# Per-head norm with the log read from PSUM, and a guard before the second up weight load, in a decoder trunk on one core

## Chip, cores and metric

One Trainium2 (trn2) chip, one core. The metric is device time in microseconds (us) of one execution of the program. Times of the whole kernel are the median over runs; durations of single instructions come from one execution that the hardware profiler recorded.

## What is computed

One decoder layer over 1024 tokens of width 1024, all in float32. Cut to what matters:

```
h = rms_norm(x, norm_mix_g);  z = h @ w_in                 # 512 pooling columns, then q, k, v of 4 heads
y_pool = pooling_mixer(z[..., :512])                       # trailing windows 2, 4, 8, 16, then a map per group
o = diff_attention(q, k, v, lam, rel_bias)                 # two softmax maps per head, 128 value channels per head
o = rms_norm(o, subln_g, 1e-5) * (1.0 - lam_init)          # the per-head norm, over the 128 channels of a head
x = x + concat(y_pool, o) @ w_out
h = rms_norm(x, norm_ffn_g);  gu = h @ ffn_w_in            # 2 x 2816 columns
x = x + (silu(causal_conv3(gu[:, :2816])) * gu[:, 2816:]) @ ffn_w_out
out = rms_norm(x, norm_final_g)
```

## The kernel before

All matrix products are made in two-part precision: an operand is split into a rounded part (hi) and the rest (lo), and three matmuls (hi x hi, hi x lo, lo x hi) stand for one. The split is a cast on ScalarE (lines 79 and 83) and a subtraction on GpSimd or VectorE (lines 80 and 84). P is 128.

The kernel runs in stages. Row norms of x and transposes come first, then the projections of q, k, v and of the pooling groups, interleaved with attention by a list written out by hand (`PLAN`, line 37). `attention(h, j)` (line 373) does 256 tokens of head h: two softmax maps, transposes, the split of the weights (ah, al), and the product with v into the PSUM tile "pv". The kernel keeps eight PSUM tiles (lines 65 to 75): three "sc", two "tp", two "mm" and a single "pv", called a bank below. At every odd j, 512 tokens of the head are complete, and their per-head norm follows (lines 411 to 430): a Square on ScalarE, a split, two matmuls with a matrix of ones that put the sum of squares on all partitions (tile ss, also in the "pv" bank), the variance, r = exp(-0.5 ln(variance)), one Newton step for r on VectorE, and the scaling of yT by r and gsub. There are eight such norms.

Then the output projection runs in three groups of channel blocks (`OUT_PLAN`, line 39); the rows wander through device memory (x1_d) between the groups. In the third group (lines 602 to 610) each row tile t is finished, normed by `norm2(t)` (line 577 scales it in place), and each pair of row tiles is turned into seven blocks (b11, b21, b22, t1 to t4) by `pair_blocks` (line 587): subtractions on GpSimd, for the last pair mostly on VectorE, then transposes on TensorE and splits. These blocks are operands of a Strassen-like scheme: for each of 22 channel tiles `ffn_up` (line 656) makes seven products of 12 matmuls, in the order 1, 6, 7, 5, 2, 4, 3. `up_weights(ct)` (line 616) loads the two weight tiles ru and rg of a channel tile into two buffers ("rw", line 619), issues both on SP's queue (line 621), forms their sums and differences on GpSimd and VectorE (lines 628 to 631) and splits them. It is called for tile ct + 1 before the products of tile ct, and for tile 0 before the loop (lines 689 to 694). The tiles gt and the split of sb take the four "x" buffers that held the row tiles. At the end comes the down projection `ffn_down`, with the last norm in `finish`.

The program is written without explicit order among engines: `TileContext(nc, schedule_with_timeline_sim=True)` (line 822) orders each engine's instructions when the program is built, by priority and by a simulated timeline, and sets the semaphores. Once built, each engine runs its instructions in that fixed order. A `tc.high_priority()` block is put ahead where it can be.

Of the kernel before, what the change touches and what calls it, by code (L numbers as in the profile page):

```python
# [9 lines left out]
F32 = mybir.dt.float32  # L10
F32R = mybir.dt.float32r
AF = mybir.ActivationFunctionType
ALU = mybir.AluOpType
PSUM = bass.MemoryType.PSUM

P = 128
S = 1024
D = 1024
KC = D // P
NT = S // P  # L20
# [5 lines left out]
SUB_EPS = 1e-5  # L26
LAM_INIT = 0.8 - 0.6 * math.exp(-0.3 * 0)
# [15 lines left out]
def trunk_kernel(ctx, tc, x, norm_mix_g, w_in, pool_w, rows, line, rel_bias, w_out, norm_ffn_g,  # L43
                 ffn_w_in, ffn_w_out, norm_final_g, onehot, out):
    nc = tc.nc
# [7 lines left out]
    const = ctx.enter_context(tc.tile_pool(name="const", bufs=1))  # L53
# [5 lines left out]
    att = st_att.enter_context(tc.tile_pool(name="att", bufs=1))  # L59
    ps_a = ctx.enter_context(tc.tile_pool(name="ps_a", bufs=1, space=PSUM))  # L60

    def slot(dt, name):
        return slots.tile([P, S], dt, tag="y", name=name)

    def sc_ps(name):
        return ps_a.tile([P, 512], F32, tag="sc", bufs=3, name=name)
# [121 lines left out]
    prm = const.tile([P, 96], F32, name="prm")  # L188
    gsub = const.tile([P, 1], F32, name="gsub")
    nlam = const.tile([P, 1], F32, name="nlam")  # L190

    def small_params():
        r_ps = sc_ps("r_ps")
        nc.tensor.matmul(r_ps[0:NH, :], rb, oh, start=True, stop=True)
        r_sb = att.tile([NH, 512], F32, tag="vt", bufs=1, name="r_sb")
        nc.vector.tensor_copy(r_sb, r_ps[0:NH, :])
        nc.sync.dma_start(scratch, r_sb)
        prm_ps = sc_ps("prm_ps")
        nc.tensor.transpose(prm_ps[:, 0:93], prow[0:93, :], ident[0:93, 0:93])
        nc.vector.tensor_copy(prm[:, 0:93], prm_ps[:, 0:93])  # L200
        nc.vector.tensor_scalar(gsub, prm[:, 92:93], 1.0 - LAM_INIT, None, op0=ALU.mult)
        nc.vector.tensor_copy(recfar, flat[:, 256:276])
        lam_s = const.tile([P, 2], F32, name="lam_s")
        lam_p = att.tile([P, 64], F32, tag="tb", bufs=1, name="lam_p")
        for j in range(2):
            nc.vector.tensor_tensor_reduce(lam_p, lam_in[:, 2 * j, :], lam_in[:, 2 * j + 1, :], 1.0, 0.0,
                                           ALU.mult, ALU.add, lam_s[:, j:j + 1])
        lam_e = const.tile([P, 2], F32, name="lam_e")
        nc.scalar.activation(lam_e, lam_s, AF.Exp)
        nc.vector.tensor_tensor(nlam, lam_e[:, 1:2], lam_e[:, 0:1], op=ALU.subtract)  # L210
        nc.vector.tensor_scalar(nlam, nlam, -LAM_INIT, None, op0=ALU.add)
# [109 lines left out]
    for t in range(NT):  # L321
# [9 lines left out]
        sq = att.tile([P, S], F32, tag="pl", bufs=3, name=f"sq_{t}")  # L331
        r = row_rstd(xt, sq, f"m{t}")
# [40 lines left out]
    def attention(h, j):  # L373
        tb, (q, kh, kl, vh, vl) = bias[h], qkv[h]
        if j == 0:
            yT[4 + h] = slot(F32, f"yT{4 + h}")
        y = yT[4 + h]
        a = []
        for i in (2 * j, 2 * j + 1):
            w = (i + 1) * P  # L380
            negm = small.tile([P, 2], F32, tag="negm", name=f"nm{h}_{i}")
            sums = small.tile([P, 2], F32, tag="sums", name=f"sm{h}_{i}")
            s = [att.tile([P, S], F32, tag="p", bufs=4, name=f"p{h}_{i}_{c}") for c in range(2)]
            for c in range(2):
                softmax_map(h, tb, i, c, q, kh, kl, s[c], negm, sums)
            r = small.tile([P, 2], F32, tag="rcp", name=f"rc{h}_{i}")
            nc.vector.reciprocal(r, sums)
            nc.vector.tensor_scalar(r[:, 1:2], r[:, 1:2], nlam, None, op0=ALU.mult)
            nc.scalar.mul(s[1][:, 0:w], s[1][:, 0:w], r[:, 1:2])
            nc.vector.scalar_tensor_tensor(s[0][:, 0:w], s[0][:, 0:w], r[:, 0:1], s[1][:, 0:w],  # L390
                                           op0=ALU.mult, op1=ALU.add)
            if i % 2 == 0:
                nc.gpsimd.memset(s[0][:, w:w + P], 0.0)
            a.append(s[0])
        nk = 2 * j + 2
        pv = pv_ps(f"pv{h}_{j}")
        for kp in range(nk // 2):
            tp = tp_ps(f"tpa{h}_{j}_{kp}")
            for u in range(2):
                for v in range(2):  # L400
                    k = 2 * kp + u
                    nc.tensor.transpose(tp[:, 2 * u + v, :], a[v][:, k * P:(k + 1) * P], ident)  # L402
            ah = att.tile([P, 4, P], F32R, tag="ah", bufs=2, name=f"ah{h}_{j}_{kp}")
            al = att.tile([P, 4, P], F32R, tag="al", bufs=2, name=f"al{h}_{j}_{kp}")
            psplit(ah, al, tp)
            for u in range(2):
                k = 2 * kp + u
                mm3(pv[:, 0:256], vh[:, k, :], vl[:, k, :], ah[:, 2 * u:2 * u + 2, :],
                    al[:, 2 * u:2 * u + 2, :], k == 0, k == nk - 1)
        nc.scalar.copy(y[:, j * 256:(j + 1) * 256], pv[:, 0:256])  # L410
        if j % 2:
            cs = slice((j // 2) * 512, (j // 2) * 512 + 512)
            n = f"{h}_{j}"
            sq = att.tile([P, 512], F32, tag="ln", bufs=2, name=f"sq{n}")
            nc.scalar.activation(sq, y[:, cs], AF.Square)
            sh = att.tile([P, 512], F32R, tag="ah", bufs=2, name=f"sqh{n}")
            sl = att.tile([P, 512], F32R, tag="al", bufs=2, name=f"sql{n}")
            split(sh, sl, sq)
            ss = pv_ps(f"ss{n}")
            nc.tensor.matmul(ss, ones, sh, start=True, stop=False)  # L420
            nc.tensor.matmul(ss, ones, sl, start=False, stop=True)
            var = att.tile([P, 512], F32, tag="ln", bufs=2, name=f"va{n}")
            nc.vector.tensor_scalar(var, ss, 1.0 / P, SUB_EPS, op0=ALU.mult, op1=ALU.add)
            r = att.tile([P, 512], F32, tag="al", bufs=2, name=f"r{n}")
            nc.scalar.activation(r, var, AF.Ln)
            nc.scalar.activation(r, r, AF.Exp, scale=-0.5)
            nc.vector.tensor_tensor(sq, r, r, op=ALU.mult)
            nc.vector.scalar_tensor_tensor(sq, sq, -0.5, var, op0=ALU.mult, op1=ALU.mult)
            nc.vector.scalar_tensor_tensor(r, sq, 1.5, r, op0=ALU.add, op1=ALU.mult)
            nc.vector.scalar_tensor_tensor(y[:, cs], y[:, cs], gsub, r, op0=ALU.mult, op1=ALU.mult)  # L430


# [54 lines left out]
    bias = {}  # L487
# [40 lines left out]
    x1 = [None] * NT  # L528
# [87 lines left out]
    def up_weights(ct):  # L616
        raw = []
        for n, c in (("u", NCT + ct), ("g", ct)):
            r = mid.tile([P, KC * P], F32, tag="rw", bufs=2, name=f"r{n}{ct}")
            src = ffn_w_in[:, c * P:(c + 1) * P].rearrange("(k p) c -> p k c", p=P)  # L620
            nc.sync.dma_start(r.rearrange("p (k c) -> p k c", c=P), src)
            raw.append(r)
        u, g = raw
        a11, a12, a21, a22 = u[:, 0:512], u[:, 512:1024], g[:, 0:512], g[:, 512:1024]
        sa = mid.tile([P, S], F32, tag="st", bufs=2, name=f"sa{ct}")
        sb = mid.tile([P, S], F32, tag="st", bufs=2, name=f"sb{ct}")
        s1, s2, s3, s4 = sa[:, 0:512], sa[:, 512:1024], sb[:, 0:512], sb[:, 512:1024]
        nc.gpsimd.tensor_tensor(s1, a21, a22, op=ALU.add)  # L628
        nc.vector.tensor_tensor(s2, s1, a11, op=ALU.subtract)  # L629
        nc.vector.tensor_tensor(s4, a12, s2, op=ALU.subtract)  # L630
        nc.gpsimd.tensor_tensor(s3, a11, a21, op=ALU.subtract)
        uh, ul = u_tile(F32R, f"uh{ct}"), u_tile(F32R, f"ul{ct}")
        split(uh, ul, u)
        gt = x_tile(F32R, f"gt{ct}")
        split(gt[:, 0:512], gt[:, 512:1024], a22, nc.vector)
        sh = []
        for n, t in (("a", sa), ("b", sb)):
            h, l = (u_tile if n == "a" else x_tile)(F32R, f"s{n}h{ct}"), u_tile(F32R, f"s{n}l{ct}")
            split(h, l, t, nc.vector)
            sh.append((blocks(h), blocks(l)))  # L640
        (ah, al), (bh_, bl_), (uh, ul), gb = sh[0], sh[1], (blocks(uh), blocks(ul)), blocks(gt)
        return {"1": (uh[:, 0], ul[:, 0], "b11"), "2": (uh[:, 1], ul[:, 1], "b21"), "3": (bh_[:, 1], bl_[:, 1], "b22"),
                "4": (gb[:, 0], gb[:, 1], "t4"), "5": (ah[:, 0], al[:, 0], "t1"), "6": (ah[:, 1], al[:, 1], "t2"),
                "7": (bh_[:, 0], bl_[:, 0], "t3")}
# [112 lines left out]
    ct = 0  # L757
# [68 lines left out]
```

## Time and profile before

| | |
|---|---|
| median of 3 runs | 1113.54 us |
| lowest and highest run | 1113.40 and 1116.36 us |
| the profiled execution | 1115.49 us |
| its span in the profile | 1113.7 us |
| TensorE granted clock, mean over the span | 0.987 |

Engines are named PE (TensorE matmul), PEld (its weight load), DVE (VectorE), ACT (ScalarE), POOL (GpSimd) and SP (SyncE, which here only issues transfers); a q behind a name is that engine's queue. Times within the span count from its start. A line number such as L621 is the line of the kernel that issued an instruction; where a helper issues it, as the splits on lines 79, 80, 83 and 84, the tile names tell which use it is. "out<-in" gives the tiles, without their numbers. What stands in brackets at the end of a row of the timeline is how long the engine was idle before the instruction, and what ended that.

### The profile page before, as it was taken

To read this page: it belongs to the slowest core of one execution; us is meant where nothing else is said; L and a number is where in the kernel's file an instruction comes from. 1 tells how busy PE (TensorE), PEld (TensorE's weight loads), DVE (VectorE), ACT (ScalarE), POOL (GpSimd) and SP (SyncE) were. 2 spreads that over 40 slices of the span, in tenths; PEclk is the share of its full clock that TensorE was granted. 3 is DMA by queue.
4 is the path that set the end of the run, shared out by engine and by line. 5 is a ranking of instruction groups with operands and counts; after the bars stand their busy time and mean duration, and the time that the engine had idled before them with its cause. 6 is when DMAs were issued, how large, how long until landed. Compare 5 with 4: busy or idle time off the path is not lost.

```text
span 1113.7 us, 13597 instructions
## 1 busy us (share of the span) xinstructions
PE 1066.6 (96%) x5011; PEld 884.0 (79%) x5011; DVE 732.3 (66%) x1213; ACT 475.9 (43%) x775; POOL 341.7 (31%) x240
## 2 busy tenths in 40 slices
PE   5999999999899997999999999999999999999997
PEld 4988888887677675878888888888888788888885
DVE  7556787877797689577657656755665655544545
ACT  5557476655752355244333443443344222111133
POOL 3232242433730247133312232221314322221211
PEclk9999999999899998999999999999999999999999
DMA  8010110110386742123122212222247632212112
GB/s 242 28 50 27 43 46 19 43 39 26 133 278 216 242 171 76 57 95 95 57 94 95 93 59 96 90 81 76 82 127 267 223 114 99 89 60 95 39 50 102
DMA packets 85990, 111.76 MB, mean 100 GB/s; under 512 B 3618, under 2 KB 66303, under 8 KB 85924
## 3 DMA queue, kind: packets, MB, share of 16 engines
q1 hardware_dynamic: 79300, 86.78, 24.4%
q10 hardware_dynamic: 6624, 24.12, 5.5%
q8 instruction: 39, 0.64, 0.2%
q14 instruction: 27, 0.22, 0.1%
HBM read 82.57 MB, written 28.32 MB: 100 GB/s over the span
## 4 chain that ended last, share of the span: by engine, by line
PE 81%; DVE 8%; issue 4%; DMA 3%; ACT 1%; POOL 1%; SPq 1%; DVEq 0%; ACTq 0%; POOLq 0%
PE p L650 36%; PE fo L747 7%; PE fo L749 7%; PE fo L748 7%; PE tpa L402 1%; PE z_q L144 1%; PE z_q L145 1%; PE z_q L143 1%; PE o L538 1%; PE o L539 1%; PE o L540 1%; PE z_p L143 1%; PE z_p L144 1%; PE z_p L145 1%; PE z_v L143 1%
## 5 line engine op out<-in xcount | busy, mean ns | idle before, releaser
L747 PE MATMUL fo<-w,a 128*128 128x512 f32 x352 | 137.3, 390 | 2.8 <-DVE xr L750 2.8
L750 DVE TENSOR_TENSOR xr<-xr,fo 128x512 f32<-128x512 f32 x112 | 75.9, 684 | 97.0 <-PE fo L749 96.3
L748 PE MATMUL fo<-w,a 128*128 128x512 f32 x352 | 137.0, 389 | 0.0
L749 PE MATMUL fo<-w,a 128*128 128x512 f32 x352 | 137.0, 389 | 0.0
L80 POOL TENSOR_TENSOR w<-rw,w 128x1024 fp32r<-128x1024 f32 x22 | 61.3, 2796 | 156.4 <-ACT w L79 151.1
L628 POOL TENSOR_TENSOR sa<-rg 128x512 f32<-128x512 f32 x22 | 32.9, 1495 | 209.8 <-DMA rg<-in_ffn_w_in_dram 201.3
L80 POOL TENSOR_TENSOR ul<-ru,uh 128x1024 fp32r<-128x1024 f32 x22 | 58.1, 2642 | 71.8 <-PE p L650 37.6
L747 PEld LDWEIGHTS fo<-w,a 128*128 128x128 f32 x352 | 66.1, 188 | 17.6 <-DVE xr L750 4.0
L749 PEld LDWEIGHTS fo<-w,a 128*128 128x128 f32 x352 | 66.1, 188 | 13.9
L748 PEld LDWEIGHTS fo<-w,a 128*128 128x128 f32 x352 | 66.1, 188 | 13.6
L79 ACT CAST a<-ra 128x1024 fp32r<-128x1024 f32 x22 | 23.1, 1051 | 118.8 <-DVE xr L750 64.1
L362 ACT ACTIVATE p<-p,nm 128x128 f32<-128x128 f32 (+7 forms) x64 | 49.6, 776 | 40.9 <-DVE nm L361 40.5
L650 PE MATMUL p<-t4h,gt 128*128 128x512 f32 x176 | 58.9, 396 | 1.7 <-DVE g L675 1.7
L629 DVE TENSOR_TENSOR sa<-sa,ru 128x512 f32<-128x512 f32 x22 | 39.9, 1814 | 21.1 <-POOL sa L628 21.1
L538 PE MATMUL o<-woh,yh 128*128 128x512 f32 x128 | 51.9, 409 | 1.6 <-DVE x L541 1.4
L349 POOL CAST qz<-q 64x128 fp32r<-64x128 f32 x64 | 24.5, 384 | 92.3 <-PE s L353 85.4
L79 ACT CAST uh<-ru 128x1024 fp32r<-128x1024 f32 x22 | 23.2, 1054 | 68.0 <-PE p L650 67.4
L539 PE MATMUL o<-wol,yh 128*128 128x512 f32 x128 | 50.6, 397 | 1.4 <-POOL wol L80 1.4
L677 DVE TENSOR_TENSOR g<-eb,p 128x512 f32<-128x512 f32 x22 | 15.1, 687 | 55.5 <-PE p L650 55.5
L80 DVE TENSOR_TENSOR a<-ra,a 128x1024 fp32r<-128x1024 f32 x22 | 43.0, 1956 | 12.1 <-ACT a L79 11.6
L540 PE MATMUL o<-woh,yl 128*128 128x512 f32 x128 | 50.0, 393 | 0.9 <-DVE yl L80 0.9
L79 ACT CAST gt<-rg 128x512 fp32r<-128x512 f32 x22 | 13.7, 623 | 82.1 <-PE p L650 75.1
(264 smaller groups left out, 3111.0 us busy)
## 6 DMA issues: line engine op xcount, KB each, us to landing
x_rows<-x ACTq DMA_DIRECT2D x24, 512.0 KB, 3.6
ru<-in_ffn_w_in_dram SPq DMA_DIRECT2D x22, 512.0 KB, 4.0
rg<-in_ffn_w_in_dram SPq DMA_DIRECT2D x22, 512.0 KB, 3.9
act_rows<-cv ACTq DMA_DIRECT2D x22, 512.0 KB, 2.6
rw<-in_ffn_w_out_dram SPq DMA_DIRECT2D x22, 512.0 KB, 4.4
ra<-act_rows SPq DMA_DIRECT2D x22, 512.0 KB, 3.4
x<-in_x_dram SPq DMA_DIRECT2D x16, 512.0 KB, 5.6
x<-x_rows SPq DMA_DIRECT2D x16, 512.0 KB, 3.7
```

The costliest lines, as they stand in the source:

```text
L79: nc.scalar.copy(hi, src)
L80: (lo_eng or nc.gpsimd).tensor_tensor(lo, src, hi.bitcast(F32), op=ALU.subtract)
L362: nc.scalar.activation(s[:, 0:w], s[:, 0:w], AF.Exp, bias=negm[:, c:c + 1], accum_out=sums[:, c:c + 1])
L538: nc.tensor.matmul(ps, yh[:, ts], wh[:, cs], start=n == 0, stop=False)
L539: nc.tensor.matmul(ps, yh[:, ts], wl[:, cs], start=False, stop=False)
L540: nc.tensor.matmul(ps, yl[:, ts], wh[:, cs], start=False, stop=n == len(wo) - 1)
L629: nc.vector.tensor_tensor(s2, s1, a11, op=ALU.subtract)
L650: nc.tensor.matmul(ps, w[:, k, :], h[:, k, :], start=start and k == 0 and n == 0, stop=k == 3 and n == 2, skip_group_check=not start)
L747: nc.tensor.matmul(ps, ah[:, ts], wh[:, cs], start=n == 0, stop=False)
L748: nc.tensor.matmul(ps, ah[:, ts], wl[:, cs], start=False, stop=False)
L749: nc.tensor.matmul(ps, al[:, ts], wh[:, cs], start=False, stop=n == len(ops) - 1)
L750: nc.vector.tensor_tensor(xr[t][:, cs], xr[t][:, cs], ps, op=ALU.add)
```

## The change

In the per-head norm the variance is no longer made on VectorE. The log reads the sum of squares from PSUM, with the scale 1/P and the small constant as a bias from a new one-column tile, eps_s. The square of r is made on ScalarE, with a scale such that it comes out as 0.5 r^2 / P. The Newton step is then (ss + P eps) * sq, and (that - 1.5) * r, which has the opposite sign; gsub takes the sign back. The tile for the variance is gone. In `up_weights`, for the second channel tile alone, a one-column copy from the last column of the last row tile into each of the two weight buffers stands ahead of its load, so that the load waits for the copy and the copy for the norm of that row tile.

```
+    eps_s = const.tile([P, 1], F32, name="eps_s")
+    nc.vector.memset(eps_s, SUB_EPS)
...
-        nc.vector.tensor_scalar(gsub, prm[:, 92:93], 1.0 - LAM_INIT, None, op0=ALU.mult)
+        nc.vector.tensor_scalar(gsub, prm[:, 92:93], LAM_INIT - 1.0, None, op0=ALU.mult)
...
-            var = att.tile([P, 512], F32, tag="ln", bufs=2, name=f"va{n}")
-            nc.vector.tensor_scalar(var, ss, 1.0 / P, SUB_EPS, op0=ALU.mult, op1=ALU.add)
             r = att.tile([P, 512], F32, tag="al", bufs=2, name=f"r{n}")
-            nc.scalar.activation(r, var, AF.Ln)
+            nc.scalar.activation(r, ss, AF.Ln, bias=eps_s, scale=1.0 / P)
             nc.scalar.activation(r, r, AF.Exp, scale=-0.5)
-            nc.vector.tensor_tensor(sq, r, r, op=ALU.mult)
-            nc.vector.scalar_tensor_tensor(sq, sq, -0.5, var, op0=ALU.mult, op1=ALU.mult)
-            nc.vector.scalar_tensor_tensor(r, sq, 1.5, r, op0=ALU.add, op1=ALU.mult)
+            nc.scalar.activation(sq, r, AF.Square, scale=(0.5 / P) ** 0.5)
+            nc.vector.scalar_tensor_tensor(sq, ss, SUB_EPS * P, sq, op0=ALU.add, op1=ALU.mult)
+            nc.vector.scalar_tensor_tensor(r, sq, 1.5, r, op0=ALU.subtract, op1=ALU.mult)
             nc.vector.scalar_tensor_tensor(y[:, cs], y[:, cs], gsub, r, op0=ALU.mult, op1=ALU.mult)
...
             r = mid.tile([P, KC * P], F32, tag="rw", bufs=2, name=f"r{n}{ct}")
+            if ct == 1:
+                nc.vector.tensor_copy(r[:, 0:1], x1[NT - 1][:, D - 1:D])
             src = ffn_w_in[:, c * P:(c + 1) * P].rearrange("(k p) c -> p k c", p=P)
```

## Rows read from the trace of the kernel before

**Rows 1.** Busy time of each engine over the span, share of it, instructions

```profile
PE 1066.6 (96%) x5011; PEld 884.0 (79%) x5011; DVE 732.3 (66%) x1213; ACT 475.9 (43%) x775; POOL 341.7 (31%) x240
```

**Rows 2.** Busy time by stage, with instructions, granted clock, DMA share, GB/s

```profile
core 0: us, PE busy (x) PEld busy (x) DVE busy (x) ACT busy (x) POOL busy (x), PEclk, DMA share, GB/s
250.00:300.00 50.00, 43.84 (x216) 36.20 (x215) 37.80 (x90) 33.75 (x63) 29.06 (x24) 0.90 0.22 78
300.00:340.00 40.00, 37.42 (x189) 30.19 (x188) 38.22 (x79) 21.47 (x37) 13.58 (x11) 1.00 0.72 252
430.00:485.00 55.00, 50.31 (x219) 40.53 (x220) 41.40 (x45) 23.23 (x32) 23.96 (x13) 0.93 0.20 59
485.00:855.00 370.00, 370.00 (x1627) 306.07 (x1626) 235.42 (x237) 149.36 (x178) 102.40 (x57) 1.00 0.31 98
```

**Rows 3.** Single lines: ns min/median/max, first and last start, forms

```profile
L423 DVE TENSOR_SCALAR va<-ss x8: 676/685/694, 103.2 to 371.1; 128x512 f32<-128x512 f32 x8
...
L427 DVE TENSOR_TENSOR sq<-r x8: 667/682/693, 107.1 to 373.3; 128x512 f32<-128x512 f32 x8
...
L428 DVE SCALAR_TENSOR_TENSOR sq<-sq,va x8: 674/691/2283, 107.8 to 374.1; 128x512 f32<-128x512 f32 x8
...
L415 ACT ACTIVATE sq<-yT x8: 614/631/634, 97.7 to 364.5; 128x512 f32<-128x512 f32 x8
...
L84 DVE TENSOR_TENSOR al<-tpa,ah x40: 672/680/693, 74.8 to 359.4; 128x512 fp32r<-128x512 f32 x40
...
L702 DVE COPY xr<-sbh x8: 143/153/154, 840.8 to 859.2; 128x1 f32<-128x1 f32 x8
```

**Rows 4.** Timeline near the start: start us, duration us, engine, line

```profile
5.48 0.15 DVE L118 TENSOR_SCALAR var_m<-ss_m 128x1 f32<-128x1 f32 x1 [3.35 <-ACT sq L116]
```

**Rows 5.** Timeline of the stretch 303 to 337, norms of two heads

```profile
303.91 0.69 DVE L423 TENSOR_SCALAR va<-ss 128x512 f32<-128x512 f32 x1
...
333.60 2.45 POOL L80 TENSOR_TENSOR wol<-wo,woh 128x1024 fp32r<-128x1024 f32 x1 [5.48 <-ACT woh L79]
...
334.32 2.28 DVE L428 SCALAR_TENSOR_TENSOR sq<-sq,va 128x512 f32<-128x512 f32 x1
```

**Rows 6.** Timeline of the stretch 376 to 384, TensorE after the last norm

```profile
382.47 0.50 PE L539 MATMUL o<-wol,yh 128*128 128x512 f32 x1 [1.01 <-POOL wol L80]
...
383.55 0.50 PE L540 MATMUL o<-woh,yl 128*128 128x512 f32 x1 [0.59 <-DVE yl L80]
```

**Rows 7.** Timeline of the stretch 256 to 266, the norm at 258 us

```profile
258.48 0.69 DVE L423 TENSOR_SCALAR va<-ss 128x512 f32<-128x512 f32 x1 [0.81 <-PE ss L421]
...
261.14 0.38 PE L143 MATMUL pv<-ah,vh 128*128 128x256 f32 x1 [1.22 <-ACT ah L83]
...
263.40 0.64 ACT L426 ACTIVATE r<-r 128x512 f32<-128x512 f32 x1
```

**Rows 8.** Timeline of the stretch 430 to 445, the last row norm and pair

```profile
431.59 0.38 SPq L621 DMA_DIRECT2D ru<-in_ffn_w_in_dram  x1
...
434.54 1.70 DVE L577 SCALAR_TENSOR_TENSOR x<-x,rr_f,g_ffn 128x1024 f32<-128x1024 f32 x1
...
436.87 0.38 SPq L621 DMA_DIRECT2D rg<-in_ffn_w_in_dram  x1
...
438.73 3.16 POOL L80 TENSOR_TENSOR ul<-ru,uh 128x1024 fp32r<-128x1024 f32 x1 [0.73 <-ACT uh L79]
...
439.61 2.84 DVE L596 TENSOR_TENSOR ta<-x,ta 128x512 f32<-128x512 f32 x1
...
443.19 0.75 PE L584 MATMUL tp_t<-ident,tb 128*128 128x128 f32 x4 [2.49 <-DVE t2l L84]
```

**Rows 9.** Timeline of the stretch 470 to 484, the stop in the first tiles

```profile
473.64 0.37 SPq L621 DMA_DIRECT2D rg<-in_ffn_w_in_dram  x1
...
479.51 2.88 DVE L629 TENSOR_TENSOR sa<-sa,ru 128x512 f32<-128x512 f32 x1
...
483.04 0.50 PE L650 MATMUL p<-t4h,gt 128*128 128x512 f32 x1 [1.74 <-DVE g L675]
```

**Rows 10.** Busy time of the stretch 480 to 490, columns as in rows 2

```profile
480.00:490.00 10.00, 8.26 (x29) 6.32 (x28) 8.12 (x9) 3.82 (x4) 3.53 (x2) 0.83 0.50 156
```

## Prediction

> **What bounds the kernel now.** I read the profile from the whole to the part: the busy table first, then busy time by stage, then the gaps in front of single instructions. The busy table [rows 1] has TensorE busy for 1066.6 us of a span of 1113.7, VectorE for 732.3 and ScalarE for 475.9. So there are 47 us in which TensorE has nothing, and a change that takes no work from TensorE can only gain there, or where its clock is low. The stages [rows 2] say where: from 485 to 855 us TensorE is busy for all of 370 us at clock 1.00, and nothing that happens on VectorE shortens it. Idle time stands in the later attention stages: 6.16 us from 250 to 300 (clock 0.90), 2.58 from 300 to 340, and 4.69 from 430 to 485 (clock 0.93). In 300 to 340 VectorE is busy for 38.22 of 40 us: there it sets the pace. The reader should see in this that the same VectorE pass is worth nothing in one stage and nearly its whole length in another.
>
> **The norm, pass by pass.** Each of the eight norms (four heads, two halves) now has five VectorE passes [rows 3]: the variance from PSUM (0.685 us), the square of r (0.682), the product (0.691, at most 2.283), and the two that stay. The change drops the first two and gives ScalarE a Square of the same shape as line 415 (0.631). VectorE is relieved of 8 x (0.685 + 0.682) = 10.9 us, ScalarE gets 8 x 0.631 = 5.0 us more. Along the chain of one norm the variance and the square (1.367) go and the Square (0.631) comes: 0.74 us shorter, and one handover less. Changing the sign of gsub and of the constant costs nothing: the instructions are the same in number and shape. The new memset of one column falls into the 3.35 us in which VectorE waits for the first sum of squares [rows 4]; without that cover it would cost about what the one-column pass after that wait takes, 0.15 us.
>
> What is that worth? Four of the eight norms lie before 250 us, and another in a stage with slack; where TensorE is full I count zero. Two lie in the stretch paced by VectorE (the variance pass of one starts at 303.91, the product of the other at 334.32 [rows 5]). They lose 4 x 0.68 = 2.7 us of passes, and the second has the product that took 2.28 us while GpSimd ran a 2.45 us subtraction beside it. In the new form that product reads one operand from PSUM; the row for a pass of two operands, one from PSUM, is the split of the attention weights (line 84, al), 680 ns in the median and at most 693 over 40 [rows 3], as short as a pass from SBUF alone, so up to 1.6 us more could go. But the stage has only 2.58 us of idle TensorE. Ends 0 and 2.6; I take **1.6**, nearer to the upper end because VectorE is at 96%. [...]
>
> The last norm, of head 3, sits on the chain of waits: its scaling of yT is followed by the split of yT, and TensorE waits 0.59 us for that split at 383.55 [rows 6]. 0.74 us off the chain comes through if nothing else ends later, but a moment before (382.47) TensorE waits 1.01 us for the split of an output weight on GpSimd, which no norm shortens. Ends 0 and 1.6 (both waits); I take **0.7**.
>
> **The bank that is held longer.** The sum of squares lies in the single "pv" bank. Now the variance pass frees it; afterwards it is read by the log and again by the product, after Ln, Exp and Square. What queues behind it is the next attention block's pv matmul, in TensorE's fixed order. For the norm at 258 us the bank is free at 259.17 and pv starts at 261.14 [rows 7]; Exp runs at 263.40, so the product could not end before about 263.40 + 0.64 + 0.63 + 0.69 = 265.4. That is 4.2 us late, if TensorE has nothing else to run; it has the projection of k, which the order can put ahead, and at 261.14 it came late already, after 1.22 us of waiting for the cast of the weights. Ends 0 and 4.2 lost; I take **0.7 lost**, near the lower end, since the order is made anew at build with this wait known.
>
> **The second up weight load.** Two one-column copies on VectorE now stand between the last row norm and the two loads on SP's queue. Their nearest row is the same guard before the reload of x1: 0.153 us each [rows 3], behind the row norm on the same engine; queued behind them are the last pair's subtractions, 0.3 us later at most. Now the load of ru for the second channel tile is issued at 431.59, that of rg at 436.87; the last row norm runs from 434.54 to 436.24 [rows 8]. So ru moves by 4.9 us and rg by almost nothing. Behind the two issues on SP's queue stand only the loads of the third tile, which wait for these buffers in any case; GpSimd's split ul (438.73, 3.16 us) moves to about 442. What does that do? The subtraction of the last pair on VectorE (line 596) took 2.84 us beside that split, against 0.68 for the nearest two-operand pass: up to 2.16 us sooner. But TensorE, which waited 2.49 us for line 84 behind it, loses the second tile's product 1, which it now runs early with uh. Twelve matmuls at 0.227 us (370 us / 1627 in the full stage [rows 2]) are 2.7 us of work no longer there to fill the wait. Ends +2.2 and -4.9 (the whole delay of ru); I take **0**.
>
> After that the two tiles no longer interleave. Now TensorE stops at 481.30 for 1.74 us, for a g that sits on VectorE behind line 629 (2.88 us), which comes after a load issued only at 473.64 [rows 9]; that load waits for a buffer which the first tile's late products hold. If the first tile runs to its end before the second starts, its 60 matmuls after b11 and b21 (seven products of 12, less two) end some 13.6 us after 444, near 458, well before that load, and the stop has no cause. [...] Ends 0 and 3.4; I take **3.4**, because the chain that causes it starts with the interleaving.
>
> **Sum.** 1.6 + 0.7 - 0.7 + 0 + 3.4 = 5.0 us. The profiled execution took 1115.49 us with a span of 1113.7; with the change 1110.5 and 1108.7. It stands 1.95 us above the median of the runs, 1113.54, so for the median 1108.5.
>
> **Rivals.**
> *It is hidden.* The passes come off VectorE where TensorE was fed anyway, and a new wait takes the place of the one at 481. For it: four of eight norms lie under a full TensorE, and the order of all engines is made anew at build. Against it: VectorE at 38.22 of 40 us. Then 1 us of the 5.0 is left: 1112.5.
> *The handover gains more.* VectorE's passes with two SBUF operands grow while GpSimd works (0.69 to 2.28 [rows 3, 5]); with ul gone from beside line 596, the 2.16 us comes through in full, and some 1.7 more from the low clock that follows the wait (3.4 - 1.74, what it costs after the stop at 481). 1108.5 - 3.8 = 1104.7. [...]
> *Slower: the load comes too late.* One mechanism: ru lands 4.9 us later, and with it uh, ul and the sums of the second tile, while the first tile's products depend on the last pair, so that TensorE has neither. It decides if the last pair's blocks are not ready when the first tile's b11 and b21 products end (about 440 us). Then the whole 4.9 us is lost with 1.7 at the low clock as above, against 2.3 gained in the norms: 1113.54 + 4.3 = 1117.8. For it: the wait of 2.49 us at 440.7 shows that TensorE is dry there already. Against it: it is dry on VectorE's account, which gets relief.
> *The wait does not bind*, being met before the buffer comes free. ru was issued at 431.59, rg at 436.87, the norm ends at 436.24, so it binds for ru alone; if the new order brings the norm forward, only the norms' 1.6 counts: 1111.9, part of the hidden case.
>
> **How the numbers follow.** Forecast 0.45, handover gains more 0.13, hidden (with the wait that does not bind) 0.28, slower 0.14. A measurement of this kernel can tell about 0.3%, 3.3 us, from no change. Faster takes the first and second: 0.58; same is the hidden case, 0.28; slower 0.14. The range reaches from 1103.5, the second case with 1.2 us of the larger gain in the norms, to 1115, the hidden case with the bank costing 2.5 us more; the slower case is left out. The likeliest case's own range is 1105.5 to 1110.
>
> **What would show it.** In the changed profile: lines 423 and 427 gone from VectorE, its busy time some 11 us less, ScalarE's 5 more; the product at 0.69 us everywhere; VectorE clearly under 38 of 40 us around 300 to 340 and TensorE's gaps there smaller; no gap in front of pv longer than 1 us after a norm; ru's second load right after the last row norm; no stop near 480. I am wrong if TensorE stands idle longer than 5 us together between 436 and 450, or if 485 to 855 is no longer full.

## The result, and the profile after

The changed kernel is slower: 1128.4 us, median of 4 runs (1121.87 to 1131.33), against 1114.08 us for the kernel before in the same session (4 runs). The ratio is 1.0123, 95% interval 1.0098 to 1.0147. The forecast was 1108.5 us, the range ended at 1115.0. The profiled execution of the changed kernel is its fastest run, 1121.87 us with a span of 1120.1. The others show a mean granted clock of 0.985 or 0.986 where this one shows 0.991; 0.0055 of 1126 us is an estimated 6.2 us, close to the 6.4 and 6.7 us by which two of the others are longer (the third by 9.5). Its line numbers are two higher from the new tile to the norm (L421 is L423) and again behind the guard (L650 is L652).

The busy table, beside [rows 1]:

```profile
PE 1074.7 (96%) x5011; PEld 880.4 (79%) x5011; DVE 710.0 (63%) x1200; ACT 481.4 (43%) x783; POOL 335.5 (30%) x240
```

VectorE lost 22.3 us, ScalarE gained 5.5. TensorE, with the same 5011 matmuls, is busy 8 us longer. The stages say where, with the columns of [rows 2]:

```profile
250.00:300.00 50.00, 43.87 (x228) 36.51 (x227) 33.65 (x85) 32.42 (x61) 24.74 (x24) 0.91 0.24 85
300.00:340.00 40.00, 35.79 (x183) 29.12 (x182) 34.49 (x83) 22.56 (x38) 12.79 (x10) 0.99 0.67 222
...
430.00:485.00 55.00, 49.40 (x223) 38.93 (x222) 38.31 (x45) 23.45 (x32) 21.56 (x12) 0.99 0.24 69
485.00:855.00 370.00, 370.00 (x1588) 297.16 (x1587) 229.54 (x230) 144.64 (x174) 101.09 (x56) 1.00 0.29 92
...
480.00:490.00 10.00, 9.17 (x39) 7.42 (x40) 8.62 (x11) 5.04 (x6) 2.65 (x2) 1.00 0.50 157
```

The reader should look at the number in brackets from 485 to 855 us. TensorE is busy for 370.00 of 370 us at a granted clock of 1.00 in both kernels, but it does 1588 matmuls where it did 1627 [rows 2]: 233.0 ns for each in place of 227.4. No gap, no wait and no lower clock shows in this stage; each matmul takes longer. Up to it the changed kernel was ahead: up product 252 starts at 497.7 us, before at 501.1. The last one starts at 873.8, before at 866.6. (An up product is here and below one matmul of the up phase, 22 x 7 x 12 = 1848 of them, counted from 0; each of the 22 channel tiles has 84.)

Only some matmuls are slow, in the same microseconds. The timeline of TensorE where the last up products (L652) and the first down products (L749 to L751) take turns; first column the start, second the duration:

```profile
867.47 0.39 PE L750 MATMUL fo<-w,a 128*128 128x512 f32 x1
867.70 0.39 PE L751 MATMUL fo<-w,a 128*128 128x512 f32 x1
867.93 0.39 PE L749 MATMUL fo<-w,a 128*128 128x512 f32 x1
...
868.86 0.39 PE L652 MATMUL p<-b22h,sbl 128*128 128x512 f32 x1
869.09 0.40 PE L652 MATMUL p<-b22h,sbh 128*128 128x512 f32 x1
869.32 0.39 PE L652 MATMUL p<-b22l,sbh 128*128 128x512 f32 x1
869.55 0.40 PE L652 MATMUL p<-b22h,sbl 128*128 128x512 f32 x1
869.79 0.39 PE L652 MATMUL p<-b22h,sbh 128*128 128x512 f32 x1
```

Rounded to 0.01 us the rows hardly show it, the mean does: where the two take turns, from 864.5 to 873.8 us, the down products start 226.7 ns apart and the up products 233.3. Over all starts that follow each other within 300 ns, the mean interval of the down products is 226.8 ns before and 226.7 after, that of the up products 226.8 before and 233.3 after. 1848 x 6.5 ns is 12.0 us: most of the loss.

The parts that the prediction costed one by one. The norm's three passes on VectorE (groups of instructions: busy us, mean ns, idle time before), then the square on ScalarE (ns min/median/max, first and last start):

```profile
L430 DVE SCALAR_TENSOR_TENSOR yT<-yT,gsub,r 128x512 f32<-128x512 f32 x8 | 7.0, 874 | 0.0
L429 DVE SCALAR_TENSOR_TENSOR r<-sq,r 128x512 f32<-128x512 f32 x8 | 5.7, 708 | 0.0
L428 DVE SCALAR_TENSOR_TENSOR sq<-ss,sq 128x512 f32<-128x512 f32 x8 | 5.5, 682 | 0.2
```

```profile
L427 ACT ACTIVATE sq<-r x8: 614/632/643, 108.7 to 369.9; 128x512 f32<-128x512 f32 x8
```

And the timeline of the new memset, the guard, the loads behind it, and the stop near 481:

```profile
0.95 0.06 DVE L192 MEMSET eps_s<- 128x1 f32 x1
...
431.14 1.28 DVE L577 SCALAR_TENSOR_TENSOR x<-x,rr_f,g_ffn 128x1024 f32<-128x1024 f32 x1
...
434.02 0.14 DVE L621 COPY ru<-x 128x1 f32<-128x1 f32 x1
...
434.29 0.38 SPq L623 DMA_DIRECT2D ru<-in_ffn_w_in_dram  x1
...
434.90 0.41 SPq L623 DMA_DIRECT2D rg<-in_ffn_w_in_dram  x1
...
436.92 0.68 DVE L596 TENSOR_TENSOR ta<-x,ta 128x512 f32<-128x512 f32 x1
...
439.41 2.37 POOL L80 TENSOR_TENSOR ul<-ru,uh 128x1024 fp32r<-128x1024 f32 x1 [3.49 <-ACT uh L79]
...
471.42 0.37 SPq L623 DMA_DIRECT2D rg<-in_ffn_w_in_dram  x1
...
480.83 0.50 PE L652 MATMUL p<-t4h,gt 128*128 128x512 f32 x1 [1.49 <-DVE g L677]
```

The memset takes 0.06 us at the very start. The loads now stand behind the guard, 2.7 us later for ru and 2.0 earlier for rg than in [rows 8]. The stop is still there [rows 9].

### The profile page after: what moved, and what is told of

Read it like the earlier page. It is cut to its first block, busy times and chain, and to the rows that moved or that the text cites. A ratio compares the mean times of both kernels' runs of the same rounds, so it can differ in the third digit from the quotient of the medians.

```text
span 1120.1 us, 13594 instructions
## 1 busy us (share of the span) xinstructions
PE 1074.7 (96%) x5011; PEld 880.4 (79%) x5011; DVE 710.0 (63%) x1200; ACT 481.4 (43%) x783; POOL 335.5 (30%) x240
## 4 chain that ended last, share of the span: by engine, by line
PE 79%; DVE 8%; issue 4%; ACT 3%; DMA 2%; POOL 1%; SPq 1%; DVEq 0%; ACTq 0%; POOLq 0%
PE p L652 36%; PE fo L749 7%; PE fo L751 7%; PE fo L750 7%; PE o L539 2%; PE o L540 2%; PE o L538 2%; PE z_p L144 1%; PE z_p L143 1%; PE z_p L145 1%; PE z_k L143 1%; PE z_k L145 1%; PE z_k L144 1%; PE tpa L404 1%; PE s L354 1%
## 5 line engine op out<-in xcount | busy, mean ns | idle before, releaser
L749 PE MATMUL fo<-w,a 128*128 128x512 f32 x352 | 137.3, 390 | 2.1 <-DVE xr L752 2.0
L751 PE MATMUL fo<-w,a 128*128 128x512 f32 x352 | 137.0, 389 | 0.0
L749 PEld LDWEIGHTS fo<-w,a 128*128 128x128 f32 x352 | 66.1, 188 | 16.8 <-DVE xr L752 3.3
L751 PEld LDWEIGHTS fo<-w,a 128*128 128x128 f32 x352 | 66.1, 188 | 13.8
L79 ACT CAST a<-ra 128x1024 fp32r<-128x1024 f32 x22 | 23.0, 1046 | 120.5 <-DVE xr L752 64.2
L652 PE MATMUL p<-t4h,gt 128*128 128x512 f32 x176 | 59.0, 396 | 1.5 <-DVE g L677 1.5
```

The costliest lines, as they stand in the source:

```text
L79: nc.scalar.copy(hi, src)
L652: nc.tensor.matmul(ps, w[:, k, :], h[:, k, :], start=start and k == 0 and n == 0, stop=k == 3 and n == 2, skip_group_check=not start)
L749: nc.tensor.matmul(ps, ah[:, ts], wh[:, cs], start=n == 0, stop=False)
L751: nc.tensor.matmul(ps, al[:, ts], wh[:, cs], start=False, stop=n == len(ops) - 1)
```

## The experiments

**What the memset's tile does.** Apart from rotating buffers that come in another order, whole multiples of 2048 bytes away, the addresses of the built programs (bytes within a partition) differ in one way. eps_s is placed 32 bytes behind nlam, and all tiles that are allocated behind it on that side move by 32: the blocks b11h, t4h, b22h, the projection weights, and w and a of the down phase. The tiles allocated from the other side (uh, gt, sbh, hTh) stay. In a row such as p<-b11h,uh the first tile is the moving operand, the 128x512 that the matmul's row gives, and the second the stationary one, 128 x 128 values for which the trace has a weight load of its own on PEld (188 ns in the median before, the first at 428.9 us, its matmul at 429.0):

```
                          before    after   after, eps_s in nlam's slot
nlam                       18592    18592    18592
eps_s                          -    18624    in nlam's slot
b11h (moving, up)          20192    20224    20192
uh   (stationary, up)     200672   200672   200672
uh - b11h              705 x 256  705 x 256 - 32   705 x 256
a    (down)                44768    44800    44768
w    (down)                52960    52992    52960
```

So the theory: the time of a matmul depends on where its two operands lie relative to each other. In the up phase the address of one is shifted and that of the other is not; in the down phase both are shifted alike. The rivals: the new order of the instructions, the guard, or the norm itself. The first four kernels were made to tell these apart.

*1. The changed kernel with eps_s in a 64-byte slot.*

```
-    eps_s = const.tile([P, 1], F32, name="eps_s")
+    eps_s = const.tile([P, 16], F32, name="eps_s")[:, 0:1]
```

> The changed kernel with eps_s 64 bytes wide in place of 4 (its slot is 64 bytes, not 32), the same instructions in the same order on every engine. Theory A (placement): the new 32-byte slot moved every tile of the left side of SBUF by 32 bytes against those of the right side, and a matmul whose two operands then differ modulo 64 starts 233 ns after the one before instead of 227; with 64 bytes they agree again, so the up matmuls go back to 226.8 ns and the kernel to 1107 us (1105 to 1110), 0.5% faster than the kernel before. Theory B (the new waits and the new order cost the time): order and waits are the same, so the time stays at 1122 to 1131 us and the interval at 233. Theory C (the chip gave a lower clock): granted clock and time as in the changed kernel, whatever the addresses.

Measured: 1119.44 us, ratio 1.0056 [1.0041, 1.0071], up products 228.9 ns apart, with the instruction order of the changed kernel unchanged. The stage from 510 to 850 us, first in the kernel before, then here:

```profile
510.00:850.00 340.00, 340.00 (x1501) 281.38 (x1500) 217.06 (x218) 136.01 (x163) 95.64 (x53) 1.00 0.30 95
```

```profile
510.00:850.00 340.00, 340.00 (x1487) 278.92 (x1486) 216.40 (x217) 135.40 (x162) 94.84 (x52) 1.00 0.28 91
```

It shows 340 / 1487 = 228.6 ns. The size of a tile that nothing else uses changes the ratio from 1.0123 to 1.0056, some 7.5 us. The expected 226.8 ns and 1107 us did not come: 64 bytes off are better than 32 and worse than none.

*2. The kernel before, with nothing but nlam's slot grown to 64 bytes, so that the same tiles move by 32.*

```
-    nlam = const.tile([P, 1], F32, name="nlam")
+    nlam = const.tile([P, 16], F32, name="nlam")[:, 0:1]
```

> The kernel before with nlam in a slot of 64 bytes, which moves the left side by 32 bytes as the change did, nothing else. Theory A: up matmuls at 233 ns, projections at 232; 1056 down matmuls unchanged at 227; 1848 x 6.5 ns = 12 us and some 3 us from the earlier stages, so 1126 to 1129 us, 1.2% slower. Theory B and C: 1113.5 us and 227 ns as before.

Measured: 1127.67 us, ratio 1.0130 [1.0111, 1.0149], up products 233.3 ns apart.

```profile
510.00:850.00 340.00, 340.00 (x1459) 273.13 (x1458) 214.47 (x211) 133.40 (x158) 93.17 (x52) 1.00 0.26 86
```

This has neither the norm nor the guard and on every engine the order of before, and it is as slow as the changed kernel (ratio 1.0123). Norm, guard and order are not needed for the loss.

*3. The kernel before with the guard alone*, nothing moved:

```
+            if ct == 1:
+                nc.vector.tensor_copy(r[:, 0:1], x1[NT - 1][:, D - 1:D])
```

> The kernel before with the guard of the second up weight load alone; no new tile, so no address moves. Theory A says nothing of it beyond 227 ns everywhere. The prediction's step (stop near 480 goes, 3.4 us): 1110 us. If the guard only trades one wait for another: 1112 to 1115. If it is what made the change slow (theory B): over 1120.

Measured: 1113.32 us, ratio 1.0007 [0.9995, 1.0020]. The guard alone is worth nothing that can be measured; the expected step to 1110 did not come, and the stop near 481 us is there, 1.73 us.

*4. The changed kernel without the guard, eps_s in the 64-byte slot* (the two lines of the guard taken out of number 1).

> The changed norm without the guard, with eps_s 64 bytes wide so that the operands agree as before. Theory A: up matmuls at 227 ns; the norm's own gain as predicted is 1.6 + 0.7 - 0.7 = 1.6 us, so 1112 us; if the norm carries the 5 us that the changed kernel was ahead by the first up tiles, 1108. Theory B with the norm as its cause: over 1120.

Measured: 1123.25 us, ratio 1.0092 [1.0076, 1.0108], up products 228.9 ns apart as in number 1, so neither expected time (1112, 1108) could come. Without the guard it is 3.8 us slower than with it, where the guard alone was worth nothing.

*5. The whole change with the constant in the second column of nlam's tile*, so that nothing moves; *7* is the same without the guard.

```
-    nlam = const.tile([P, 1], F32, name="nlam")
-    eps_s = const.tile([P, 1], F32, name="eps_s")
+    nlam_eps = const.tile([P, 2], F32, name="nlam_eps")
+    nlam, eps_s = nlam_eps[:, 0:1], nlam_eps[:, 1:2]
```

> The whole change, with eps_s in the second column of nlam's 32-byte slot, so that no tile of SBUF moves against the kernel before; instructions and order are those of the changed kernel. Theory A, mended (what counts is the offset between a matmul's two operands; 0 as before is 227 ns, +32 bytes 233, +64 bytes 229): up matmuls at 226.8 ns, projections at 228, and 1119.4 us of the 64-byte kernel less 1848 x 2.1 ns and some 960 x 4.5 ns = 8 us, so 1111 us (1109 to 1113). Theory B (the 64-byte kernel is slow by its waits): 1119 us.

> The norm alone, without the guard, eps_s again in nlam's slot, nothing moved. Theory A: 1123.25 us of the 64-byte form less 8: 1115 us, so the norm by itself gains nothing or costs 2 us, and the guard pays only together with it. The prediction's sizes for the norm (1.6 us gained) would give 1111. Theory B: 1123.

Measured: number 5 takes 1114.49 us, ratio 1.0012 [1.0000, 1.0024]; number 7 takes 1118.36 us, 1.0058 [1.0039, 1.0077]. Both have up products 226.8 ns apart. The stage in number 5:

```profile
510.00:850.00 340.00, 340.00 (x1501) 281.52 (x1501) 216.32 (x218) 136.33 (x163) 94.37 (x53) 1.00 0.30 97
```

1501 is the count of the kernel before in the same 340 us. The same arithmetic in the same order as the changed kernel takes 13.9 us less (12.4 by the ratios, each to the kernel before of its session) when one column of a constant lies elsewhere. What is left is that the whole change, with the placement undone, gains nothing, where 1109 to 1113 was expected; and number 7, expected at 1115, is slower than the kernel before.

*6. The kernel before with nlam's slot so large that the tiles move by 128*; *8. the kernel before with a 32-byte pad on the other side*, so that uh, gt, sbh and hTh move and the rest stays.

```
-    nlam = const.tile([P, 1], F32, name="nlam")
+    nlam = const.tile([P, 40], F32, name="nlam")[:, 0:1]
```

```
+    padr = ctx.enter_context(tc.tile_pool(name="padr", bufs=1, side="right"))
+    nc.vector.memset(padr.tile([P, 8], F32, name="pad"), 0.0)
```

> The kernel before with the left side moved by 128 bytes (nlam in a slot of 160), nothing else. Theory A says that the interval depends on the offset alone: if the pattern repeats every 128 bytes, 226.8 ns and 1112.7 us; if it repeats later or falls off with distance, between 227 and 229 ns and 1113 to 1121 us. Theory B and C: 1112.7 us.

> The kernel before with the right side of SBUF moved down by 32 bytes by a pad there and one memset more (0.1 us at the start, beside the first load); the left side stays. Theory A, the offset between the operands: it is +32 again, as in the changed kernel, so up matmuls at 233.3 ns and 1127.7 us. Theory A', that the left tiles' own addresses count: 226.8 ns and 1112.7 us.

Measured: number 6 takes 1123.84 us, ratio 1.0098 [1.0083, 1.0112], 232.4 ns; number 8 takes 1126.59 us, 1.0124 [1.0111, 1.0138], 233.3 ns. Number 6 lies outside both expectations: 128 bytes off is neither like 0 nor nearer to it than 64. The stage of number 6, then that of number 8:

```profile
510.00:850.00 340.00, 340.00 (x1465) 276.03 (x1464) 215.16 (x212) 133.87 (x159) 91.15 (x52) 1.00 0.27 86
```

```profile
510.00:850.00 340.00, 340.00 (x1459) 273.55 (x1458) 214.61 (x212) 133.31 (x158) 91.92 (x52) 1.00 0.27 86
```

In number 8 the moving operand lies where it lay before and the stationary one is 32 bytes lower; in number 2 the moving one is 32 higher. The distance is the same and so is the interval, 233.3 ns. It is the distance that counts (both sides were moved for 32 bytes only). That it is the distance to the other operand, and not to some other tile, the down phase of number 2 bears out: w and a are shifted there against xr, rw and ra, which stay, and keep 226.8 ns. Over all profiles (mean interval between starts, ns):

```
bytes off a multiple of 256:         0       32       64      128
up products                        226.8    233.3    228.9    232.4
projections                        228.1    232.0    232.7    231.6
down products (both moved)         226.8    226.8    226.8    226.8
```

*9. The kernel before once more*, for a second profile, because 3.4 us of the prediction hung on one stop.

> The kernel before, unchanged, profiled a second time. It asks whether the stop of 1.74 us at 481 us and the 3.4 us that the prediction put on it belong to the kernel or to that one execution, which at 1115.49 us was above the median of its runs. If they belong to the kernel: a gap of some 1.7 us near 481 again, low clock behind it, and 252 minus 168 products of the up phase 22.7 us apart again. If to the execution: no gap over 0.5 us there, the same stretch in 21.3 us, as in the kernel before with its buffers shifted, and a span some 2 us below 1113.7. The interval between up matmuls should be 226.8 ns either way.

Measured, in one execution: 1113.91 us, span 1112.1, up products 226.8 ns apart. The stop is there again, the low clock behind it is not:

```profile
483.30 0.50 PE L650 MATMUL p<-t4h,gt 128*128 128x512 f32 x1 [1.74 <-DVE g L675]
```

```profile
480.00:490.00 10.00, 8.26 (x36) 6.50 (x36) 9.38 (x10) 4.63 (x5) 3.78 (x2) 1.00 0.48 155
```

TensorE does 36 matmuls at a granted clock of 1.00, where [rows 10] has 29 at 0.83. The two expectations split: the stop belongs to the kernel, the low clock behind it, 0.50 from 484.5 to 487.9 us in the first profile, does not come each time. Nor is it a thing of that one execution: in number 6, which has the order of the kernel before, the stop (1.77 us, to 486.39) has it again:

```profile
485.00:495.00 10.00, 8.61 (x30) 6.91 (x31) 7.79 (x10) 3.83 (x4) 2.69 (x3) 0.83 0.51 157
```

All 14 profiles of this case have the stop, 1.49 to 1.90 us long; these two have the low clock right behind it.

*10. Number 7 with the square of r back on VectorE*, scaled there; *11* is the same with the guard.

```
-            nc.scalar.activation(sq, r, AF.Square, scale=(0.5 / P) ** 0.5)
+            nc.vector.scalar_tensor_tensor(sq, r, 0.5 / P, r, op0=ALU.mult, op1=ALU.mult)
```

> The norm of the change with the constant in the second column of an existing tile, no guard, and the square of r put back on VectorE, scaled there, so that one of the two saved passes stays saved (the variance). Nothing is moved, so up matmuls start 226.8 ns apart. If the loss of the norm alone at unmoved operands (1.0058 with the square on ScalarE) comes from ScalarE's additional pass or from the shorter norm as such, this version lies between: 1.000 to 1.004. If it comes from the order that is made anew and happens to feed the last pair later, it follows the order and not the passes: then the time is set by the stretch from the first up product to the 84th, 35.9 us with the square on ScalarE and 30.4 before, and can be anywhere from 0.998 to 1.008. The attention's last transposes should start between 355.8 us (norm with Square on ScalarE) and 358.2 us (before).

> The whole change, with the constant in an existing slot (nothing moved) and the square of r back on VectorE: two passes become one, not two passes fewer. If the guard does what it did for the norm with Square on ScalarE (first up product to the 84th 35.9 us without, 31.9 with it), this stretch shrinks from 35.5 to about 31.5 us and the time falls from 1108.3 to about 1104, 0.991 to 0.993 of the kernel before. If the guard only matters for the one order that it was tried with, the time stays at 1107 to 1110. Attention should end as without the guard, last transposes near 349.5 us, last output product near 412.5.

Measured: number 10 takes 1108.28 us, ratio 0.9958 [0.9944, 0.9972]. Number 11 takes 1105.58 us, ratio 0.9920 [0.9906, 0.9934]: faster than both kernels. Most of the gain, 6.6 of 8.2 us, has its place: the attention's last transposes start at 351.6 us against 358.2, and up product 84 at 452.8 against 459.4; from there on it runs as in the second profile of the kernel before. Number 10 came out below both expected ranges. Number 11 came where the guard's gain would put it, but its profile does not show that gain: up product 84 starts at 452.8 us in both, profiled at 1106.91 and 1106.81 us. A wait at the handover to the up phase shrank by 3.1 us, first number 10, then number 11, while attention ended 2.1 us later:

```profile
437.75 0.87 PE L584 MATMUL tp_t<-ident,tb 128*128 128x128 f32 x4 [4.36 <-DVE t1l L84]
```

```profile
437.86 1.12 PE L584 MATMUL tp_t<-ident,tb 128*128 128x128 f32 x4 [1.29 <-DVE t1l L84]
```

*12. The kernel before with the square alone on ScalarE*, the variance still on VectorE:

```
-            nc.vector.tensor_tensor(sq, r, r, op=ALU.mult)
+            nc.scalar.activation(sq, r, AF.Square)
```

> The kernel before with the other half of the norm's edit alone: the square of r goes to ScalarE, the variance pass stays on VectorE, no constant tile, no guard, nothing moved. If ScalarE's additional pass is what spoils the gain of the norm (its queue holds the cast of yT, which VectorE waited 4.87 us for at 326 us in the norm with Square), this version has such a wait too and stands at or above before: 1.002 to 1.008, last transposes of attention later than 355 us. If the pass is harmless and the loss lay in the order drawn for that one version, one VectorE pass fewer per norm should show as in the version with the square back: 0.995 to 0.999.

Measured: 1107.62 us, ratio 0.9945 [0.9920, 0.9969], with a wide spread: 1101.77 to 1113.06 over 11 runs, at a mean granted clock of 0.996 to 0.988; the profiled one, 1112.65, is near the slow end. So ScalarE's pass by itself does not make the kernel slower. By the medians each half of the norm's edit gains half a per cent, and the two together, number 7, lose as much.

The trace shows where they stand. The timeline of ScalarE in the changed kernel, then in number 10:

```profile
324.83 1.05 ACT L79 CAST woh<-wo 128x1024 fp32r<-128x1024 f32 x1 [5.13 <-DMA wo<-in_w_out_dram]
...
325.78 0.68 ACT L425 ACTIVATE r<-ss,eps_s 128x512 f32<-128x512 f32 x1
326.36 1.03 ACT L79 CAST yh<-yT 128x1024 fp32r<-128x1024 f32 x1
```

```profile
317.52 1.05 ACT L79 CAST woh<-wo 128x1024 fp32r<-128x1024 f32 x1
318.48 1.04 ACT L79 CAST yh<-yT 128x1024 fp32r<-128x1024 f32 x1
...
320.76 0.69 ACT L425 ACTIVATE r<-ss,nlam_eps 128x512 f32<-128x512 f32 x1 [0.28 <-PE ss L423]
```

With both edits ScalarE stands 5.13 us (5.48 and 5.80 in numbers 5 and 7) at the cast of an output weight that has not landed, and behind it wait the log of a norm and the cast of yT. TensorE then stands 3.42 us at 326.63 in the changed kernel, 3.78 in number 5, 4.09 in number 7, and 0.65 in number 10, each at an output product that waits for VectorE. In number 10 the weight is there when the cast's turn comes. Number 12 has a wait of 5.13 us in front of this cast too, with 4.0 us of stops on TensorE (2.68 and 1.33), and number 11, the fastest, one of 2.80 with a stop of 2.24, so the wait alone does not make the difference between a gain and a loss. In number 7 another 3.71 us goes at the handover, where a split for the last pair is late, against 1.30 with the guard; but number 10 loses 4.36 us there and is fast. First number 7, then number 5:

```profile
443.65 2.79 POOL L80 TENSOR_TENSOR ul<-ru,uh 128x1024 fp32r<-128x1024 f32 x1
...
447.65 1.11 PE L584 MATMUL tp_t<-ident,tb 128*128 128x128 f32 x4 [3.71 <-DVE t1l L84]
```

```profile
440.89 2.38 POOL L80 TENSOR_TENSOR ul<-ru,uh 128x1024 fp32r<-128x1024 f32 x1 [3.55 <-ACT uh L79]
...
444.47 0.66 PE L584 MATMUL tp_t<-ident,tb 128*128 128x128 f32 x4 [1.30 <-DVE t1l L84]
```

The granted clock differs as well: from 300 to 340 us it is 0.93 in numbers 5 and 7, 0.99 in the changed kernel and 1.00 in number 10; from 430 to 485 it is 0.91 in number 7 and 0.97 in number 10. How much of the difference is the clock was not tested.

The stages of all these versions, read from the starts of matmuls in one profile each (us):

| version | last projection | last attention transpose | up product 84 | last up product |
|---|---|---|---|---|
| before (first, second profile) | 280.3, 281.5 | 358.2, 359.6 | 459.4, 459.5 | 866.6, 865.2 |
| after | 280.1 | 355.6 | 456.8 | 873.8 |
| 5, same slot | 277.3 | 355.5 | 458.0 | 863.8 |
| 7, same slot, no guard | 277.4 | 355.8 | 463.5 | 869.2 |
| 10, square back, no guard | 274.9 | 349.5 | 452.8 | 858.5 |
| 11, square back | 274.9 | 351.6 | 452.8 | 858.5 |
| 12, square alone | 276.6 | 356.8 | 458.8 | 864.4 |

## Why the prediction was wrong

**The step that failed** is the sentence on the new memset: it "falls into the 3.35 us in which VectorE waits", and so the constant was costed at nothing. The instruction did cost nothing (0.06 us). The tile was never costed: its slot moved one operand of every up product by 32 bytes against the other, 12.0 us over 1848 products. Numbers 2 and 5 show it from both sides. A bound was at hand and was not sought: I took the 370 us in which TensorE is full as fixed, because nothing on VectorE shortens them, though any change in the time of one matmul is multiplied there by 1627. My own sign of being wrong, that 485 to 855 be no longer full, could not see it either: the stage stayed full, and only its count of instructions fell.

None of the rivals holds this mechanism. The slower one (1117.8) was for the load of ru; with operands unmoved the guard cost nothing (number 3) or gained (number 7 to number 5), so its price was not there.

**The norm, 1.6 us, and the last norm, 0.7.** The passes went as said, and by more. The eight norms took 37.3 us of VectorE before (10.4, 8.8, 7.1, 5.5 and 5.5 by pass) and 18.1 after, 19.1 less where I had 10.9 and 1.6: the two passes that stay also fell, from 10.4 to 7.0 and from 8.8 to 5.7. The product from PSUM takes 0.682 us in the median, as the row for al said (0.680). But the place was wrong. Number 5 gains 3.0 us up to the last projection (4.2 against the second profile of before), where I had counted zero. In the stretch from there to the last transposes, where I had put 1.6, it gains none: 78.2 us, before 77.9 and 78.1. The changed kernel, with the same order and a higher granted clock, takes 75.5 us there, and number 1 77.6; so between nothing and 2.4 us came through. In the changed kernel VectorE fell from 38.22 to 34.49 of 40 us from 300 to 340, but TensorE's busy time fell too, from 37.42 to 35.79. What was late next was the weight that ScalarE stood at, 5.13 us where it stood 0.72 before:

```profile
322.37 1.05 ACT L79 CAST woh<-wo 128x1024 fp32r<-128x1024 f32 x1 [0.72 <-DMA wo<-in_w_out_dram]
```

From the last transposes to the last output product it takes 64.2 us in the changed kernel, as before, and 65.8 in number 5, so the 0.7 did not come. The order of all engines is made anew at build, and each version of the norm got another one. That this is why two gains add up to a loss is argued and stays open: no version was run with the order held.

**The bank, 0.7 lost.** Not seen: no gap of the changed kernel from 250 to 350 us stands in front of a pv product, and the 1.22 us of [rows 7] are gone.

**The guard, 0.** Right for the guard alone, 1.0007 with no change inside its interval: in number 3 the load of ru moved by 5.4 us, near the 4.9 that I had, and it cost nothing. (The 3.4 below was to come from the guard as well.) Beside the new norm it is worth 3.9 us (1118.36 to 1114.49), and some 0.4% in number 11 against number 10; the wait at the handover falls from 3.71 to 1.30 us and from 4.36 to 1.29. The prediction's pieces are there: line 596 takes 0.68 us in place of 2.84, and the pass beside ul is now another (line 597, 2.41 us). So the longer pass moved and did not vanish: of these two passes of one shape, the one of 0.68 us has no GpSimd pass beside it (GpSimd is idle for 3.49 us up to 439.41), the one of 2.41 has ul.

**The stop, 3.4.** Failed at each link. The guard was to end the interleaving of the first two channel tiles, and it did not: by the built program, their products come in nearly the order of before. In the changed kernel the first row here belongs to the second tile's product 1, the next to the first tile's product 7:

```profile
439.39 0.50 PE L652 MATMUL p<-b11h,uh 128*128 128x512 f32 x1
...
441.19 0.49 PE L652 MATMUL p<-t3h,sbh 128*128 128x512 f32 x1 [0.64 <-ACT t3h L83]
```

The stop did not go either: 1.49 us in the changed kernel, with the load of rg still issued at 471.42, and 1.90 in number 5. Whether the interleaving causes it stays open, since no version was without it. No run shows 3.4 us as what the kernel pays for the stop: at 0.227 us each, the matmuls from 480 to 490 us leave an estimated 3.4 us of the 10 in the first profile of before and 1.8 in the second, at 0.233 each 0.9 in the changed kernel. Half of the 3.4 was the low clock after the stop, which the second profile of the same kernel does not have; it came in two of 14 profiles. One execution, 1.95 us above the median, was read as the rule.

The total for operands unmoved: the forecast had 5.0 us of gain, number 5 shows none (1.0012); 3.4 of the 5.0 is the stop.

## What to carry to other kernels

A new tile, however small, is a change of placement for every tile behind it (here 4 bytes a partition moved them by 32, and the kernel took 13.9 us longer than with the constant in an existing slot): before costing a change, compare the addresses of the matmul operands in the two built programs, and put small constants into slots that exist. In a stage where an engine is always busy, compare the number of instructions done in the same window and not the busy share. And take a stall, or the clock behind it, as a property of a kernel only after further profiles show it too.

## What was not expected of the hardware

In these kernels the interval between 128x512 fp32r matmuls of the up phase went with the byte distance between the stationary and the moving operand: 226.8 ns at a multiple of 256, 233.3 with 32 bytes off, 228.9 with 64, 232.4 with 128, at a granted clock of 1.00, with no wait in the trace, and for 32 bytes whichever operand was shifted. Where both were shifted together, in the down phase, it stayed at 226.7 or 226.8. Other distances, and what lies behind this, were not tried.
